# Attention weights split on VectorE, queries rotated out of PSUM, and another order of the first steps

## The chip, the cores and the metric

The kernel runs on one core of a Trainium2 chip. Its engines work beside each other, each through a fixed list of instructions: TensorE (PE, with its weight loads PEld) multiplies, VectorE (DVE), ScalarE (ACT) and GpSimd (POOL) work elementwise, and SyncE (SP) issues most transfers from memory. TensorE writes PSUM banks, from which VectorE and ScalarE read; everything else lies in SBUF. The metric is the device time of one execution in microseconds (us), as a median of several runs.

## What is computed

Two layers of a diffusion backbone over 512 latent tokens and 256 context tokens of width 1024, all in float32. Each layer modulates and normalises its input, projects it once, runs three mixers (attention, a short gated convolution, a longer convolution), merges them, and adds an MLP. The part that the change touches is modulation, projection and attention:

```python
sh1, sc1, gt1, sh2, sc2, gt2 = modulation(c, w_mod[l], b_mod[l])   # silu(c) @ w_mod + b_mod
h_lat = rmsnorm(x, g_norm1[l]) * (1.0 + sc1) + sh1
h_ctx = rmsnorm(ctx, g_norm1[l]) * (1.0 + csc1) + csh1
p_lat = h_lat @ w_in[l]
...
q_lat = apply_rope(query_heads(p_lat, q_gain[l]), cos, sin)   # 8 heads of 128, rmsnorm, rotation
k_lat, v_lat = keys_values(p_lat[..., OFF_K:OFF_SC], k_gain[l])   # 2 heads
k_lat = apply_rope(k_lat, cos, sin)
attn_lat = latent_attention(q_lat, k_lat, v_lat, k_ctx, v_ctx)   # one softmax over latent and context keys
x_new = x + gt1 * mixer_merge(p_lat, attn_lat, lp)
```

Context tokens run through the same weights; in the last layer only their keys and values are wanted.

## The kernel before

**Products in three passes.** Every float32 product is made of two-part operands: a high part rounded to TensorE's fp32r format and a low part, the rest. `mm3` (lines 152 to 156) issues high by high (L154), low by high (L155) and high by low (L156), into one bank. Weights come in units of 128 x 1024 values (512 KB). `unit` loads one into `wraw` (L121 or L123, four buffers), casts the high part on ScalarE (L125) and subtracts it for the low part on `self.lo_engine` (L127). That engine is GpSimd from the start, VectorE for V's weights and in part of a layer's rest, GpSimd again for others; in attention the four units of the first query group and the keys, and the six of the later query groups, go to GpSimd. Activations are split in the same way by `split` (ScalarE L147, VectorE or GpSimd L150).

**The first steps.** `first_modulation` makes the modulation of layer 0 in four quarters: eight loads of `w_mod` (L244, 256 KB each), products on one row (L250), a copy (L253), transposes (L256), and on VectorE the sums and the scale (L261, L263, L264). Quarter q serves the channel blocks k = 2q and 2q + 1. The blocks of x are read (L1057), squared on ScalarE (L1022), the root taken on GpSimd (`rstd`, L349 and L350) and scaled on VectorE (L1024). `modulate` transposes a channel block (L381) and evicts it with scale and shift on ScalarE (L386, L389) and VectorE (L391, L392). `qk_gemm_all` runs over k = 0 to 7, with `first_in` as the generator that is pulled ahead of each k. Its rope tables and gains are read and multiplied by `rotary` (L414, L419, L420). Layer 1 does the same from `next_in`, while layer 0's MLP ends.

**Attention.** `attention` makes keys and the first query group for the latents, then for the context, then V, then the queries of groups 1 to 3 in between the scores of the group before. A query pair comes from `qk_gemm` into one of four PSUM banks `pb`, is copied to SBUF (L405), squared on ScalarE (L457), and for latent pairs multiplied twice with the rope table on VectorE (L467) and added (L470). Each group has a third pair, the context's, in layer 0 only; it is multiplied with the gain alone (L460). Keys are then scaled on GpSimd (L500); for queries GpSimd makes the factor (L508, L510), which the softmax applies (L603 maximum, L604, L606 exponential, L607, L611). `to_heads` transposes a pair (L479). TensorE's transposes of probabilities are L625, its products with V L639 to L642.

**Order.** A scheduler fixes each engine's order ahead of the run from the program's order and its own estimates; at run time each engine works strictly through it and waits at the first instruction whose data or buffer is not there. SBUF tiles `tx` have 12 buffers, `pb` four banks here, `pa` two of double size.

Of the kernel before, what the change touches and what calls it, by code (L numbers as in the profile page):

```python
# [53 lines left out]
class Backbone:  # L54
    def __init__(self, ctx, tc, ins, out):
# [9 lines left out]
        self.lo_engine = tc.nc.gpsimd  # L65
# [50 lines left out]
    def unit(self, src, shape):  # L116
        nc = self.nc
# [4 lines left out]
        else:  # L122
            nc.sync.dma_start(out=raw, in_=src)  # L123
        hi = self.W("whi", N_SPLIT, shape, F32R)
# [274 lines left out]
    def qk_gemm(self, ws, hs, p):  # L399
        nc = self.nc  # L400
        ps = self.PB()
        for b in range(2):
            self.gemm_tm(ps[:, b * 256:(b + 1) * 256], ws, hs, 2 * p + b)
        t = self.X(512)
        nc.scalar.copy(t, ps)  # L405
        return t

    def rotary(self, l):

        nc, i = self.nc, self.i  # L410
        gains = []
# [4 lines left out]
        ropes = []  # L416
        for g in gains:
            rope = self.X(D)
            nc.sync.dma_start(out=rope, in_=i["rope"])  # L419
            nc.vector.tensor_tensor(rope.rearrange("p (q d) -> p q d", d=P), rope.rearrange("p (q d) -> p q d", d=P),  # L420
                                    g[:, None, :].broadcast_to([P, 8, P]), op=ALU.mult)
            ropes.append(rope)
        self.tables = gains, ropes

    def w_qk(self, w, u):

        src = w[u * 256:(u + 1) * 256, 0:2 * D].rearrange("(k p) (s c) -> p k s c", p=P, s=2)
        hi, lo = self.unit([src[:, k, :, 0:256] for k in range(2)], [2, 512])
# [22 lines left out]
    def qk_pair(self, ps, p, gain, rope):  # L451

        nc = self.nc
        t, t2 = ps, self.X(512)
# [7 lines left out]
        else:  # L462
            t1 = self.X(512)
            v = "p (b h d) -> p b h d"
            for dst, o in ((t1, 0), (t2, 512)):
                tab = rope[:, o + 2 * p * P:o + (2 * p + 2) * P].rearrange("p (b d) -> p b d", b=2)
                nc.vector.tensor_tensor(dst.rearrange(v, b=2, h=2), t.rearrange(v, b=2, h=2),  # L467
# [18 lines left out]
    def attention(self, l, hs, full, coming):  # L486
# [17 lines left out]
        def query(g, t, p):  # L504
            qt, qr = qs[g]
            t, ss = self.qk_pair(t, p, gains[1], ropes[1])
# [35 lines left out]
        self.lo_engine = nc.vector  # L542

        def v_heads():
            ws = self.w_rows(w, 0, OFF_V, 256)
            self.lo_engine = nc.gpsimd
# [13 lines left out]
        def queries(g):  # L560
# [3 lines left out]
            for p in range(3 if full else 2):  # L564
                query(g, self.qk_gemm(ws, hs, p), p)
# [182 lines left out]
    def layer(self, l, hs, x_src, full, last, coming):  # L748
# [208 lines left out]
        for c in range(N_FF // FF_CHUNK):  # L957
# [9 lines left out]
            for q, (h, blocks) in enumerate(orders):  # L967
# [3 lines left out]
                if q == 3:  # L971
                    self.lo_engine = nc.gpsimd
# [75 lines left out]
    def run(self):  # L1048
# [5 lines left out]
        def read(blocks):  # L1054
            xs = [self.X() for _ in blocks]
            for b, x in zip(blocks, xs):
                nc.sync.dma_start(out=x, in_=x_in(b))  # L1057
            for b, x in zip(blocks, xs):
                self.norm_in(b, x, x, self.X())

        self.read_ctx = lambda: read(range(NB_L, NB))
        self.first_cols = self.setup_cols(0)
        next(self.first_cols)
        self.quarters = [self.first_modulation(q) for q in range(4)]
        next(self.quarters[0])
        read(range(NB_L))
# [14 lines left out]
    def first_in(self, ws):  # L1081

        w = self.i["w_in"][0]
        quarters = self.quarters
        ws += self.w_qk(w, 0)
        next(quarters[1])
# [3 lines left out]
        for q in range(4):  # L1090
            if q < 2:
                next(quarters[q + 2])
            if q < 3:
# [79 lines left out]
```

## Time and profile before

| what | value |
|---|---|
| median of 3 runs | 2751.07 us (2750.91 to 2751.28) |
| the profiled execution | 2751.03 us |
| its span in the trace | 2749.2 us |
| TensorE busy | 2688.0 us (98%) |
| VectorE, ScalarE, GpSimd busy | 1625.3, 882.2, 760.5 us |
| mean granted clock of TensorE | 0.992 |

The trace covers 1.83 us less than the execution's own time. A line number is that of the kernel's file. A wait is idle time of an engine, put down to the instruction that released it last. The granted clock is given as a share of 2.4 GHz.

### The profile page before, as it was taken

The page shows a single profiled execution, that of the slowest core. Times are in us where ns is not written, and L with a number is a line of the kernel's source. Part 1 is how long each engine was busy: PE and PEld are TensorE (multiplying, and loading weights), DVE is VectorE, ACT ScalarE, POOL GpSimd, SP SyncE. Part 2 cuts the span into 40 slices and gives each one's busy share as a digit, 9 for nine tenths or more (in the row PEclk, how much of TensorE's full clock was granted, in tenths as well). Part 3 has the DMA queues.
Part 4 walks back from the last instruction along what each step waited for, and adds up shares of the span by engine and source line. Part 5 has one row for each costly group of instructions (what it writes and reads, how often), then busy time and mean ns, then how long its engine had stood idle before and what let it go on. Part 6 is the DMA issues. An engine that isn't in the chain of part 4 may idle for free.

```text
span 2749.2 us, 36048 instructions
## 1 busy us (share of the span) xinstructions
PE 2688.0 (98%) x14515; PEld 2302.1 (84%) x14515; DVE 1625.3 (59%) x2061; ACT 882.2 (32%) x1437; POOL 760.5 (28%) x621
## 2 busy tenths in 40 slices
PE   7899999999999999999999998999999999999998
PEld 4899888888888888888888887898888888888887
DVE  4557698538664434575454555667928735654445
ACT  3566222122221423412121225663223223422223
POOL 2543332233221231211110105535444212211102
PEclk9999999999999999999999999999999999999999
DMA  7111334422265243343343432113433534433332
GB/s 251 48 43 42 102 98 131 154 71 74 75 220 163 60 142 96 95 130 108 116 125 105 149 106 91 54 39 115 123 116 107 170 115 144 131 100 92 108 93 99
DMA packets 341982, 302.50 MB, mean 110 GB/s; under 512 B 10576, under 2 KB 288384, under 8 KB 341816
## 3 DMA queue, kind: packets, MB, share of 16 engines
q1 hardware_dynamic: 340400, 298.81, 35.0%
q8 instruction: 114, 1.87, 0.3%
q10 hardware_dynamic: 1416, 1.39, 0.2%
q14 instruction: 52, 0.43, 0.1%
HBM read 274.96 MB, written 25.20 MB: 109 GB/s over the span
## 4 chain that ended last, share of the span: by engine, by line
PE 89%; DVE 3%; issue 2%; ACT 1%; POOL 1%; DMA 1%; POOLq 0%; ACTq 0%; SPq 0%; DVEq 0%
PE pa L154 20%; PE pa L155 20%; PE pa L156 20%; PE pb L154 8%; PE pb L156 8%; PE pb L155 8%; PE pb L625 1%; PE pb L639 1%; PE pb L642 1%; PE pb L640 1%; DVE tx L295 1%; DMA wraw<-in_w_mod 1%; PE pb L303 1%; PE pb L479 0%; ACT tx L457 0%
## 5 line engine op out<-in xcount | busy, mean ns | idle before, releaser
L154 PE MATMUL pa<-ta,whi 128*128 128x512 f32 (+1 forms) x2912 | 1030.3, 354 | 0.8 <-DVE ta L788 0.8
L155 PE MATMUL pa<-ta,wlo 128*128 128x512 f32 (+1 forms) x2912 | 1026.1, 352 | 0.0
L156 PE MATMUL pa<-ta,whi 128*128 128x512 f32 (+1 forms) x2912 | 1025.2, 352 | 0.0
L125 ACT CAST whi<-wraw 128x1024 fp32r<-128x1024 f32 x360 | 377.6, 1050 | 1055.9 <-PE pa L156 391.6
L154 PEld LDWEIGHTS pa<-ta,whi 128*128 128x128 f32 x2912 | 551.3, 189 | 79.9 <-issue 3.4
L156 PEld LDWEIGHTS pa<-ta,whi 128*128 128x128 f32 x2912 | 550.8, 189 | 75.4 <-DVE ta L392 0.2
L155 PEld LDWEIGHTS pa<-ta,wlo 128*128 128x128 f32 x2912 | 551.4, 189 | 73.7
L127 POOL TENSOR_TENSOR wlo<-wraw,whi 128x1024 fp32r<-128x1024 f32 x138 | 334.9, 2432 | 407.4 <-ACT whi L125 358.5
L154 PE MATMUL pb<-whi,ta 128*128 128x512 f32 (+1 forms) x1200 | 434.6, 364 | 2.8 <-ACT ta L386 1.3
L155 PE MATMUL pb<-whi,ta 128*128 128x512 f32 (+1 forms) x1200 | 433.8, 361 | 2.3 <-DVE ta L392 1.8
L156 PE MATMUL pb<-wlo,ta 128*128 128x512 f32 (+1 forms) x1200 | 432.9, 361 | 1.4 <-DVE wlo L127 1.4
L707 DVE SCALAR_TENSOR_TENSOR pv<-tx,cols,pv 128x783 f32<-128x783 f32 (+1 forms) x448 | 401.2, 896 | 13.8
L127 DVE TENSOR_TENSOR wlo<-wraw,whi 128x1024 fp32r<-128x1024 f32 x222 | 294.6, 1329 | 83.6 <-ACT whi L125 78.1
L920 POOL TENSOR_TENSOR ta<-ta 128x768 fp32r<-128x768 f32 (+1 forms) x64 | 105.6, 1651 | 626.6 <-DVE ta L919 626.6
L154 PEld LDWEIGHTS pb<-whi,ta 128*128 128x128 f32 x1200 | 227.4, 190 | 41.9 <-ACT ta L386 3.0
L155 PEld LDWEIGHTS pb<-whi,ta 128*128 128x128 f32 x1200 | 227.7, 190 | 36.6 <-DVE ta L392 3.1
L156 PEld LDWEIGHTS pb<-wlo,ta 128*128 128x128 f32 x1200 | 227.2, 190 | 35.4 <-DVE wlo L127 1.9
L295 DVE SCALAR_TENSOR_TENSOR tx<-wraw,cs,tx 128x1024 f32<-128x1024 f32 x112 | 151.8, 1379 | 69.7 <-DMA wraw<-in_w_mod 64.7
L1045 DVE TENSOR_TENSOR ta<-pb,gt 128x512 f32<-128x512 f32 x100 | 68.8, 688 | 181.1 <-PE pb L156 181.0
L917 DVE TENSOR_SCALAR ta<-pa 128x768 f32<-128x768 f32 (+1 forms) x64 | 52.7, 823 | 165.2 <-PE pa L156 165.2
L745 ACT ACTIVATE ta<-pa 128x768 f32<-128x768 f32 (+1 forms) x52 | 36.6, 705 | 232.6 <-PE pa L156 232.6
L150 POOL TENSOR_TENSOR ta<-tx,ta 128x768 fp32r<-128x768 f32 (+1 forms) x32 | 53.6, 1674 | 158.4 <-ACT ta L147 154.0
(167 smaller groups left out, 2373.8 us busy)
## 6 DMA issues: line engine op xcount, KB each, us to landing
wraw<-in_w_in SPq DMA_DIRECT2D x144, 512.0 KB
wraw<-in_w_mod SPq DMA_DIRECT2D x80, 512.0 KB
wraw<-in_w_mlp_out SPq DMA_DIRECT2D x72, 512.0 KB
wraw<-in_w_mlp_in SPq DMA_DIRECT2D x64, 512.0 KB
wraw<-in_w_o SPq DMA_DIRECT2D x24, 512.0 KB
tx<-spill SPq DMA_DIRECT2D x24, 384.0 KB
ta<-in_w_mod SPq DMA_DIRECT2D x32, 256.0 KB
wraw<-in_w_attn_out SPq DMA_DIRECT2D x16, 512.0 KB
```

The costliest lines, as they stand in the source:

```text
L125: nc.scalar.copy(hi, raw)
L127: self.lo_engine.tensor_tensor(lo, raw, hi.bitcast(F32), op=ALU.subtract)
L150: (eng or nc.gpsimd).tensor_tensor(lo, src, hi.bitcast(F32), op=ALU.subtract)
L154: nc.tensor.matmul(ps, ah, bh, start=start, stop=False)
L155: nc.tensor.matmul(ps, al, bh, start=False, stop=False)
L156: nc.tensor.matmul(ps, ah, bl, start=False, stop=stop)
L295: nc.vector.scalar_tensor_tensor(acc[b], raw, c, acc[b], op0=ALU.mult, op1=ALU.add)
L707: nc.vector.scalar_tensor_tensor((v if t == K_CF - 1 else pv)[:, 0:n], u[:, t:t + n], c["cf"](t, k), (v if t == 1 else pv)[:, 0:n], op0=AL ...
L745: self.nc.scalar.activation(g[:, 0:n], ps[:, 0:n], AF.Sigmoid)
L917: nc.vector.tensor_scalar(out=v[:, 0:n], in0=ps[:, 0:n], scalar1=0.0, scalar2=None, op0=ALU.max)
L920: nc.gpsimd.tensor_tensor(lo[:, 0:n], v[:, 0:n], hi[:, 0:n].bitcast(F32), op=ALU.subtract)
L1045: nc.vector.tensor_tensor(t, ps, gt[:, o], op=ALU.mult)
```

## The change

It has four parts.

1. `lo_engine` is VectorE from the start, and no longer set to GpSimd behind V's weights: 20 L127 of attention (ten in each layer) move from GpSimd to VectorE.
2. `qk_gemm` returns the bank. The 15 copies L405 (nine in layer 0, six in layer 1) are gone; squares, rotation and the gain's multiply of these pairs read PSUM, and the result goes to a new tile.
3. SyncE reads x ahead of `w_mod`, each of the four first units of `w_in` ahead of its quarter (the first ahead of quarter 0), and both context blocks ahead of quarter 3. Before, x stood behind quarter 0, units two and three behind quarter 2, the fourth behind quarter 3, and one context block on either side of quarter 3.
4. `unit` is two functions, `load` and `halves`, and `rotary` two, so that loads are issued ahead of their splits and of the gain's multiply.

```diff
         self.bg = []
-        self.lo_engine = tc.nc.gpsimd
+        self.lo_engine = tc.nc.vector
         self.n = 0
...
     def unit(self, src, shape):
+        return self.halves(self.load(src, shape), shape)
+    def load(self, src, shape):
         nc = self.nc
...
             nc.sync.dma_start(out=raw, in_=src)
+        return raw
+    def halves(self, raw, shape):
+        nc = self.nc
         hi = self.W("whi", N_SPLIT, shape, F32R)
...
             self.gemm_tm(ps[:, b * 256:(b + 1) * 256], ws, hs, 2 * p + b)
-        t = self.X(512)
-        nc.scalar.copy(t, ps)
-        return t
+        return ps
-    def rotary(self, l):
+    def rotary_in(self, l):
         nc, i = self.nc, self.i
-        gains = []
+        gains, ropes = [], []
         for name in ("k_gain", "q_gain"):
...
             gains.append(g)
-        ropes = []
         for g in gains:
...
             nc.sync.dma_start(out=rope, in_=i["rope"])
-            nc.vector.tensor_tensor(rope.rearrange("p (q d) -> p q d", d=P), rope.rearrange("p (q d) -> p q d", d=P),
-                                    g[:, None, :].broadcast_to([P, 8, P]), op=ALU.mult)
             ropes.append(rope)
...
+    def rotary(self):
+        nc = self.nc
+        for g, rope in zip(*self.tables):
+            nc.vector.tensor_tensor(rope.rearrange("p (q d) -> p q d", d=P), rope.rearrange("p (q d) -> p q d", d=P),
+                                    g[:, None, :].broadcast_to([P, 8, P]), op=ALU.mult)
     def w_qk(self, w, u):
...
         src = w[u * 256:(u + 1) * 256, 0:2 * D].rearrange("(k p) (s c) -> p k s c", p=P, s=2)
-        hi, lo = self.unit([src[:, k, :, 0:256] for k in range(2)], [2, 512])
+        return self.load([src[:, k, :, 0:256] for k in range(2)], [2, 512])
+    def qk_halves(self, raw):
+        hi, lo = self.halves(raw, [2, 512])
         return [(hi[:, k], lo[:, k]) for k in range(2)]
...
-    def qk_pair(self, ps, p, gain, rope):
+    def qk_pair(self, ps, p, gain, rope, apart=False):
         nc = self.nc
-        t, t2 = ps, self.X(512)
+        t, t2 = self.X(512) if apart else ps, self.X(512)
         ss = self.st()
...
                 tab = rope[:, o + 2 * p * P:o + (2 * p + 2) * P].rearrange("p (b d) -> p b d", b=2)
-                nc.vector.tensor_tensor(dst.rearrange(v, b=2, h=2), t.rearrange(v, b=2, h=2),
+                nc.vector.tensor_tensor(dst.rearrange(v, b=2, h=2), ps.rearrange(v, b=2, h=2),
                                         tab[:, :, None, :].broadcast_to([P, 2, 2, P]), op=ALU.mult)
...
-        def query(g, t, p):
+        def query(g, t, p, apart=False):
             qt, qr = qs[g]
-            t, ss = self.qk_pair(t, p, gains[1], ropes[1])
+            t, ss = self.qk_pair(t, p, gains[1], ropes[1], apart)
             m = self.st()
...
-        self.lo_engine = nc.vector
         def v_heads():
             ws = self.w_rows(w, 0, OFF_V, 256)
-            self.lo_engine = nc.gpsimd
             for p in range(3):
...
             for p in range(3 if full else 2):
-                query(g, self.qk_gemm(ws, hs, p), p)
+                query(g, self.qk_gemm(ws, hs, p), p, True)
                 yield True
...
                     at = h
-                if q == 3:
-                    self.lo_engine = nc.gpsimd
                 for b in blocks:
...
                 nc.sync.dma_start(out=x, in_=x_in(b))
+            yield True
             for b, x in zip(blocks, xs):
                 self.norm_in(b, x, x, self.X())
+            yield True
-        self.read_ctx = lambda: read(range(NB_L, NB))
+        lat, self.read_ctx = read(range(NB_L)), read(range(NB_L, NB))
         self.first_cols = self.setup_cols(0)
         next(self.first_cols)
+        next(lat)
         self.quarters = [self.first_modulation(q) for q in range(4)]
-        next(self.quarters[0])
-        read(range(NB_L))
+        self.qk_raws = []
+        for q in range(2):
+            self.qk_raws.append(self.w_qk(i["w_in"][0], q))
+            next(self.quarters[q])
+        next(lat)
         next(self.first_cols)
...
         w = self.i["w_in"][0]
-        quarters = self.quarters
-        ws += self.w_qk(w, 0)
-        next(quarters[1])
+        quarters, raws = self.quarters, self.qk_raws
+        ws += self.qk_halves(raws[0])
         next(quarters[0])
...
             if q < 2:
+                raws.append(self.w_qk(w, q + 2))
                 next(quarters[q + 2])
-            if q < 3:
-                ws += self.w_qk(w, q + 1)
+            if q == 1:
+                next(self.read_ctx)
+                self.rotary_in(0)
             self.hs += self.new_pairs(2)
...
             next(self.lat)
-            if q == 1:
-                self.read_ctx()
-            if q == 2:
-                self.rotary(0)
             if q < 3:
+                ws += self.qk_halves(raws[q + 1])
                 next(quarters[q + 1])
             else:
-                run_all(self.first_cols)
+                next(self.read_ctx)
                 ctx = self.ctx_in(0)
...
                 next(quarters[q + 1])
+            else:
+                self.rotary()
+                run_all(self.first_cols)
             yield True
...
         l = DEPTH - 1
-        for u in range(KT // 2):
-            ws += self.w_qk(self.i["w_in"][l], u)
-        self.rotary(l)
+        raws = [self.w_qk(self.i["w_in"][l], u) for u in range(KT // 2)]
+        self.rotary_in(l)
+        for raw in raws:
+            ws += self.qk_halves(raw)
+        self.rotary()
         ctx = self.ctx_in(l)
```

New line numbers: L127 is now L134, L125 L132, L386 and L391 L393 and L398, L420 L431, L460 L473, L467 L480, L470 L483, L479 L492, L500 L513, L603 L613.

ScalarE in the first steps, behind the small loads of constants; L1022 are x's squares, L125 casts of weights, L386 and L389 the evictions of k = 0, 1. Before:

```order
L1022 ACTIVATE tx,st<-tx 128x1024 x4
L221 DMA tx<-in_w_cf_conv 124x128
L222 DMA tx<-in_w_cf_conv 124x128
L125 CAST whi<-wraw 128x1024
L386 ACTIVATE ta<-pa,mc_91,scale_93 128x512 x2
L389 ACTIVATE ta<-pa,mc_91,scale_93 128x512
L125 CAST whi<-wraw 128x1024 x2
L386 ACTIVATE ta<-pa,mc_91,scale_93 128x512
L1022 ACTIVATE tx,st<-tx 128x1024
L386 ACTIVATE ta<-pa,mc_91,scale_93 128x512
```

After:

```order
L1030 ACTIVATE tx,st<-tx 128x1024 x4
L228 DMA tx<-in_w_cf_conv 124x128
L229 DMA tx<-in_w_cf_conv 124x128
L132 CAST whi<-wraw 128x1024 x3
L393 ACTIVATE ta<-pa,mc_91,scale_93 128x512 x2
L396 ACTIVATE ta<-pa,mc_91,scale_93 128x512
L132 CAST whi<-wraw 128x1024
L393 ACTIVATE ta<-pa,mc_91,scale_93 128x512 x2
L396 ACTIVATE ta<-pa,mc_91,scale_93 128x512
```

Three casts now stand ahead of the first eviction, where it was one, and the fourth ahead of k = 2's.

VectorE at layer 0's first third pair; L460 is the gain's multiply, L150 the low part of transposed probabilities and other evictions, L603 the softmax maximum. Before:

```order
L150 TENSOR_TENSOR tx<-pb,tx 128x512
L604 TENSOR_SCALAR st<-st,qr 128x1
L607 RECIPROCAL st<-st 128x1
L603 TENSOR_REDUCE st<-pa 128x1
L460 TENSOR_TENSOR tx<-tx,gain 128x512
L150 TENSOR_TENSOR tx<-pb,tx 128x512
L604 TENSOR_SCALAR st<-st,qr 128x1
L150 TENSOR_TENSOR tx<-pb,tx 128x512
```

After (L473 is the multiply, L134 the splits, L157 and L613 as L150 and L603):

```order
L157 TENSOR_TENSOR tx<-pb,tx 128x512
L617 RECIPROCAL st<-st 128x1
L134 TENSOR_TENSOR wlo<-wraw,whi 128x1024 x2
L473 TENSOR_TENSOR tx<-pb,gain 128x512
L157 TENSOR_TENSOR tx<-pb,tx 128x512
L613 TENSOR_REDUCE st<-pa 128x1
L157 TENSOR_TENSOR tx<-pb,tx 128x512
L614 TENSOR_SCALAR st<-st,qr 128x1
```

Two splits of weights now stand ahead of the multiply, and the multiply reads PSUM.

GpSimd at the keys of layer 1; L500 scales a key's four parts, L349 and L350 take its root, the last four L500 are the context key's. Before:

```order
L349 TENSOR_SCALAR st<-st 128x4
L350 TENSOR_TENSOR st<-st,nhalf 128x4
L508 TENSOR_SCALAR st<-st 128x4
L510 TENSOR_TENSOR qr<-st,nhalf 128x4
L500 TENSOR_SCALAR tx<-tx,st 128x128 x4
L127 TENSOR_TENSOR wlo<-wraw,whi 128x1024
L349 TENSOR_SCALAR st<-st 128x4
L350 TENSOR_TENSOR st<-st,nhalf 128x4
L127 TENSOR_TENSOR wlo<-wraw,whi 128x1024
L500 TENSOR_SCALAR tx<-tx,st 128x128 x4
L611 TENSOR_SCALAR tx<-tx,st 128x768
L508 TENSOR_SCALAR st<-st 128x4
```

After:

```order
L356 TENSOR_SCALAR st<-st 128x4
L357 TENSOR_TENSOR st<-st,nhalf 128x4
L521 TENSOR_SCALAR st<-st 128x4
L523 TENSOR_TENSOR qr<-st,nhalf 128x4
L513 TENSOR_SCALAR tx<-tx,st 128x128 x4
L356 TENSOR_SCALAR st<-st 128x4
L357 TENSOR_TENSOR st<-st,nhalf 128x4
L513 TENSOR_SCALAR tx<-tx,st 128x128 x4
L621 TENSOR_SCALAR tx<-tx,st 128x768
L521 TENSOR_SCALAR st<-st 128x4
L523 TENSOR_TENSOR qr<-st,nhalf 128x4
```

Both splits between the second key and the context key are gone from this queue.

## Rows read from the trace of the kernel before

**Rows 1.** The page: busy time, share and instructions of each engine.

```profile
PE 2688.0 (98%) x14515; PEld 2302.1 (84%) x14515; DVE 1625.3 (59%) x2061; ACT 882.2 (32%) x1437; POOL 760.5 (28%) x621
```

**Rows 2.** TensorE's waits: engine, tile, line, released by; total us, times, longest.

```profile
PE pb L479 <- POOL tx L500: 9.2, 6, 4.4
...
PE pb L479 <- DVE tx L470: 2.8, 3, 1.6
...
PE pa L155 <- DVE ta L392: 1.3, 1, 1.3
...
PE pa L381 <- DVE ta L391: 1.2, 1, 1.2
```

**Rows 3.** Busy by stretch: PE, PEld, DVE, ACT, POOL; granted clock, DMA share, GB/s.

```profile
18.00:28.00 10.00, 4.76 (x19) 1.95 (x23) 6.38 (x11) 2.98 (x4) 4.74 (x5) 0.51 1.11 341
1690.00:1720.00 30.00, 23.85 (x170) 22.60 (x170) 11.32 (x24) 11.51 (x38) 16.29 (x21) 0.89 0.19 57
1720.00:1750.00 30.00, 26.56 (x174) 24.80 (x174) 19.11 (x36) 17.54 (x41) 19.01 (x14) 0.89 0.24 70
1706.10:1711.20 5.10, 5.10 (x26) 5.10 (x25) 0.00 (x0) 0.00 (x0) 0.00 (x0) 0.51 0.27 92
```

**Rows 4.** Groups by line and shape: busy us, mean ns, idle before.

```profile
L127 POOL TENSOR_TENSOR wlo<-wraw,whi 128x1024 fp32r<-128x1024 f32 x138 | 334.9, 2432 | 407.4 <-ACT whi L125 358.5 <-issue 42.9 <-DVE pv L707 5.3
L127 DVE TENSOR_TENSOR wlo<-wraw,whi 128x1024 fp32r<-128x1024 f32 x222 | 294.6, 1329 | 83.6 <-ACT whi L125 78.1 <-PE pb L155 0.3
...
L150 DVE TENSOR_TENSOR tx<-pb,tx 128x512 fp32r<-128x512 f32 x104 | 70.3, 685 | 13.7 <-ACT tx L147 13.4
...
L457 ACT ACTIVATE tx<-tx 128x128 f32<-128x128 f32 x104 | 30.9, 301 | 0.9
...
L470 DVE TENSOR_TENSOR tx<-tx 128x512 f32<-128x512 f32 x20 | 13.7, 686 | 0.1
...
L405 ACT COPY tx<-pb 128x512 f32<-128x512 f32 x15 | 8.8, 585 | 25.8 <-PE pb L156 17.4 <-issue 8.5
```

**Rows 5.** Timeline of the start: start us, duration us, engine, line [idle before].

```profile
20.74 2.88 DVE L1024 TENSOR_SCALAR tx<-tx,st 128x1024 f32<-128x1024 f32 x1 [0.72 <-POOL st L350]
...
26.18 0.78 ACT L386 ACTIVATE ta<-pa,mc,scale 128x512 fp32r<-128x512 f32 x1 [5.53 <-DVE scale L264]
...
35.74 1.04 ACT L125 CAST whi<-wraw 128x1024 fp32r<-128x1024 f32 x1 [0.43 <-DMA wraw<-in_w_in]
...
49.95 1.23 DVE L420 TENSOR_TENSOR tx<-tx,gain 128x1024 f32<-128x1024 f32 x1
...
28.88 1.19 PE L154 MATMUL pb<-whi,ta 128*128 128x512 f32 x4
...
50.97 0.96 PE L154 MATMUL pb<-whi,ta 128*128 128x512 f32 x3 [1.26 <-ACT ta L386]
```

**Rows 6.** Timeline of layer 0's first third pair (VectorE, GpSimd, TensorE).

```profile
143.27 0.96 DVE L603 TENSOR_REDUCE st<-pa 128x1 f32<-128x768 f32 x1 [4.37 <-PE pa L156]
144.37 2.05 DVE L460 TENSOR_TENSOR tx<-tx,gain 128x512 f32<-128x512 f32 x1
...
141.12 4.75 POOL L127 TENSOR_TENSOR wlo<-wraw,whi 128x1024 fp32r<-128x1024 f32 x2 [1.22 <-ACT whi L125]
...
147.16 0.63 PE L479 MATMUL pb<-ident,tx 128*128 128x128 f32 x4 [1.47 <-DVE st L604]
```

**Rows 7.** Timeline at the ctx key of layer 1 (GpSimd, TensorE).

```profile
1698.59 2.39 POOL L127 TENSOR_TENSOR wlo<-wraw,whi 128x1024 fp32r<-128x1024 f32 x1
...
1705.08 0.48 PE L479 MATMUL pb<-ident,tx 128*128 128x128 f32 x1 [4.43 <-POOL tx L500]
```

**Rows 8.** Timeline of layer 1's second query pair (VectorE, TensorE).

```profile
1738.47 2.72 DVE L467 TENSOR_TENSOR tx<-tx 128x512 f32<-128x512 f32 x1
...
1739.78 0.49 PE L154 MATMUL pa<-ta 128*128 128x512 f32 x1 [1.82 <-ACT tx L606]
...
1742.71 1.12 PE L479 MATMUL pb<-ident,tx 128*128 128x128 f32 x4 [1.62 <-DVE tx L470]
```

More of the change, by code (lines that the diff above doesn't have):

```diff
@@ L419, in rotary @@
             nc.sync.dma_start(out=rope, in_=i["rope"])
+            ropes.append(rope)
+        self.tables = gains, ropes
+    def rotary(self):
+        nc = self.nc
+        for g, rope in zip(*self.tables):
             nc.vector.tensor_tensor(rope.rearrange("p (q d) -> p q d", d=P), rope.rearrange("p (q d) -> p q d", d=P),
                                     g[:, None, :].broadcast_to([P, 8, P]), op=ALU.mult)
-            ropes.append(rope)
-        self.tables = gains, ropes
     def w_qk(self, w, u):
         src = w[u * 256:(u + 1) * 256, 0:2 * D].rearrange("(k p) (s c) -> p k s c", p=P, s=2)
-        hi, lo = self.unit([src[:, k, :, 0:256] for k in range(2)], [2, 512])
+        return self.load([src[:, k, :, 0:256] for k in range(2)], [2, 512])
+    def qk_halves(self, raw):
+        hi, lo = self.halves(raw, [2, 512])
         return [(hi[:, k], lo[:, k]) for k in range(2)]
```

## The prediction

> **What bounds the kernel now.** I read the page first: TensorE is busy 2688.0 of 2749.2 us [rows 1], so only 61.2 us of its idle time can be won, and the work it does is not changed. The list of TensorE's waits comes next [rows 2], to see which idle times end with something that the change touches: key heads waiting for GpSimd's multiply L500 (9.2 us in six waits, 4.4 in the longest), the pairs of heads waiting for VectorE's rotation L470, two waits behind the splits L392 and L391. Then the table by stage with the granted clock [rows 3]: in 18 to 28 us and 1706.1 to 1711.2 us the clock is 0.51, that is 1.2 GHz and not 2.4, and both follow idle time of TensorE; 1690 to 1750 us is the poorest stretch after the start, 50.41 us busy in 60. Next the prices by line and form [rows 4], last the timelines of four places [rows 5 to 8].
>
> What they show together: whenever GpSimd runs L127 (2.43 us a split [rows 4]), a VectorE operation with two SBUF operands that starts meanwhile ends with it. L1024 takes 2.88 us at 20.74 [rows 5], L460 takes 2.05 at 144.37 beside a 4.75 us pair of splits [rows 6], L467 takes 2.72 at 1738.47 [rows 8], where L470, of the same size, takes 0.69 on average [rows 4]. The trace has some ten such places.
>
> **The splits (20 from GpSimd to VectorE).** Removed on GpSimd: 20 x 2.43 = 49 us; added on VectorE: 20 x 1.33 = 27 us [rows 4]. VectorE is busy 11.32 and 19.11 us in the two stretches of 30 us from 1690 to 1750 [rows 3], so the room is there; what counts is who stands behind each. By place:
> - Layer 0's third pairs. TensorE waits 1.47 us at 147.16 behind L460, L150 and L604 [rows 6]; three such waits of 1.46 to 1.47. Now both splits stand ahead of the multiply L473. The first cast is ready at 141.1, when GpSimd starts, the second some 1.4 us later, and VectorE idles 4.37 us up to 143.27 [rows 6], so both splits are done at about 143.8, before the squares are over; the multiply takes 0.7 and not 2.05. What is left of each wait is about 0.3: -3.4 us.
> - ctx stage: the 1.3 us wait behind a stretched L392 [rows 2] goes, the V weights' splits come a little later: -1.0.
> - Boundary to layer 1: four splits in a row go from GpSimd; the 1.2 us behind L391 [rows 2] falls to 0.3: -0.9.
> - The ctx key of layer 1. GpSimd does a split, a norm, a split, and only then the four multiplies L500; TensorE waits 4.43 + 0.21 us [rows 7]. Without the two splits (2.39 and one like it) the multiplies come some 4.7 us sooner, and the order puts their transposes behind all V products as well: -4.6. The half clock follows this wait: 25 matmuls took 5.1 us there [rows 3], at full clock half, and some transposes: -3.0. I take both, since nothing else waits between 1698 and 1711.
> - 1735 to 1744 us: waits of 1.82 and 1.62 [rows 8]. The first is a softmax row maximum queued on VectorE. With the change a split (1.33) and both rotations (1.37) stand ahead of it, so it comes about 1.2 us later, while the rotated pair comes about 3 us sooner. Worked along the queue, idle falls from 3.4 to about 2.5: -1.0, and a quarter chance that the half clock of this stretch (0.89 over 30 us [rows 3], so 3.3 us lost at most) stays away: -0.7.
> - The later pairs (two waits of 1.15, the same pattern): -1.0.
>
> **Rotating out of PSUM.** 15 copies L405 of 0.585 us go from ScalarE [rows 4]. VectorE reading one PSUM operand of this size takes 0.685 (L150), both operands in SBUF 0.686 (L470) [rows 4], so I take no price; the squares at 0.301 each were timed from SBUF only; the 512-column copy from PSUM needs 0.585 for four times the columns, so the bounds are 0 to +0.1 each, hidden either way. The Trainium skill's page "VectorE: DVE Perf Modes" (Rules for kernel authors) says one should either accept the slower tier of a PSUM source or copy to SBUF first where many operations follow; three readers follow here. By it the rotation would cost more than 0.69, and the sum would rise by under 1 us for each pair; the rows of this kernel don't agree, at this size and type.
>
> The price lies elsewhere: the bank. It was free after the copy, 0.7 us; now it is free after four squares (1.3) and two rotations (1.37), which the order puts behind the squares: about 2.85 us. Four banks rotate. Counting matmuls in the new order at 0.06, 0.12 and 0.23 us for 128, 256 and 512 columns (25 of mostly 256 columns take 5.1 us at half clock [rows 3]), TensorE has 2.2 to 3.7 us of work before the bank comes round in seven of nine pairs of layer 0 (8.2 in the first, 3.1 in the second), 4.9 in four of layer 1, 2.8 and 16.5 in the others. Beyond the cover lie 0.65 + 0.65 + 0.05; with a split now and then ahead: **+2.0**. Bounds 0, and +21 with a cast (1.05) and a split (1.33) ahead of every one.
>
> **The start.** x first, each w_in unit ahead of its quarter. The stretched L1024 (2.88, [rows 5]) goes, and x is normed before the first quarter is there. Against that, ScalarE's and VectorE's order have the third unit's cast and split ahead of k=0's evictions. That unit landed at 35.7 [rows 5] and has 2 MB fewer ahead of it: 5.9 us at 341 GB/s [rows 3], and I estimate 1.7 us more since the big x transfers fill the queues sooner (0 to 3). So 28.2, cast 1.04, eviction 0.78: first product at 30.0 and not 28.88 [rows 5]; with the split and VectorE's two evictions the second kind of product is 1.7 us late. Later it wins: the stretched operations and waits at 40 to 54 us go (1.26 at 50.97 [rows 5], and some of like size). The products L431 (1.23 each, as L420 [rows 5]) now stand ahead of the third quarter's scale, and wait for the rope tables: 14.1 MB at 341 GB/s from about 5 us, 46 to 47; the scale is ready at about 49 and k=4 starts at 50.0, 1.0 before. If TensorE's clock, 0.51 until 28 us [rows 3], stays low over the first 7 us of products, 3.5 us are lost. I take **0**, between -4 (all lands sooner, clock as before) and +5.
>
> **Sum**: 0 - 1.0 - 3.4 + 2.0 - 0.9 - 7.6 - 1.7 - 1.0 = -13.6. The profiled execution took 2751.03 us, its span 2749.2 and 1.83 around it, and the median is 2751.07, so either base serves: **2737 us**.
>
> **Rivals.**
> - *The bank becomes the wait* (the slower side). In every query pair the squares find a cast ahead and the rotations a split: 5.2 us against the covers above is +21 in place of +2; the pairs' own waits (3.4) don't go, since the same queues cause them: 2737.4 + 19 + 3.4 = 2760. It decides from 1.4 us beyond the cover per pair, over 15. For it: VectorE and ScalarE work in program order and get the splits there. Against: only ten splits of a layer lie there, and VectorE idles 4.37 us ahead of the third pair [rows 6].
> - *The start and the clock don't give*: +4 at the start, and 3.0 + 0.7 of clock time not returned as other idle time of 2 us keeps TensorE slow at 1706: 2745. For it: the row of 18 to 28 us; against: no wait between 1692 and 1705 but the one that goes.
> - *The blocking turns round*: VectorE's splits now stretch GpSimd's small operations in the ctx key's chain, three times 1.33, and the clock gives back nothing there: 2737.4 + 4 + 3 = 2744. The rows show VectorE held up by GpSimd; the reverse is not among them. The Trainium skill states it as a lock: on "SBUF — State Buffer" (SBUF: two separate sides), the pair of ports that VectorE's two-operand instructions and GpSimd share goes to whichever starts first, for the whole instruction. By that rule the splits on VectorE can hold GpSimd as well; the trace agrees for the other direction, with L460's 2.05 us beside GpSimd's splits.
> - *All of it comes*: the start's -4 and both half-clock stretches: 2731.
>
> **How the numbers follow.** Forecast 0.45, all of it 0.17, start and clock 0.17, blocking 0.14, bank 0.07. The measurement tells 0.2% (5.5 us) from no change: faster is under 2745.6, slower over 2756.6. Faster: 0.45 + 0.17, half of the start rival and three quarters of the blocking one: 0.81. Slower 0.05, from the bank; the rest 0.14. The range leaves out the bank rival's far end and the best tenth: 2727 to 2750.
>
> **What would show it.** No DVE operation of two SBUF operands and 512 columns over 1 us in attention; the wait of 4.43 at the ctx key gone and the clock at 1.0 there; waits before third pairs of 0.3; TensorE's first product at about 30 us and k=4 at about 50. It is wrong if TensorE waits for L480 (bank) over 1 us in most pairs, if the ctx key's transposes still wait, or if the start is over 5 us longer.

## The result, and the profile after

The changed kernel took **2731.82 us** (median of four, 2730.98 to 2733.03) against 2751.18 (2750.91 to 2751.65): a ratio of 0.9931, with a 95% interval of 0.9918 to 0.9943. That is 19.4 us less, where 13.6 were forecast, inside the range of 2727 to 2750. The profiled execution's span is 2730.0 us against 2749.2.

The page of the changed kernel, busy time by engine, answers to [rows 1]:

```profile
PE 2682.9 (98%) x14515; PEld 2298.2 (84%) x14515; DVE 1625.6 (60%) x2081; ACT 871.7 (32%) x1422; POOL 709.2 (26%) x601
```

TensorE does the same 14515 matmuls in 5.1 us less, which I put down to the clock (the windows below), and stands idle 47.1 us and not 61.2, which is waits: 14.1 + 5.1 = 19.2, the difference of the spans. TensorE's waits, for [rows 2]:

```profile
PE pb L492 <- POOL tx L513: 4.6, 4, 1.9
...
PE pb L492 <- DVE tx L483: 1.5, 1, 1.5
```

L492 and L513 are L479 and L500 of before: 9.2 us in six waits became 4.6 in four. The stretches of [rows 3] (windows: PE, PEld, DVE, ACT, POOL; granted clock, DMA share, GB/s):

```profile
18.00:28.00 10.00, 6.30 (x27) 2.10 (x29) 2.45 (x7) 1.04 (x1) 0.00 (x0) 0.73 0.99 321
1690.00:1720.00 30.00, 29.97 (x234) 28.64 (x234) 17.51 (x37) 14.39 (x36) 12.26 (x19) 1.00 0.23 70
1720.00:1750.00 30.00, 28.15 (x213) 26.18 (x212) 21.63 (x46) 18.78 (x50) 9.76 (x12) 1.00 0.19 57
```

The 60 us from 1690 are now 58.12 us busy, at full clock. Prices by line and shape, for [rows 4]:

```profile
L134 DVE TENSOR_TENSOR wlo<-wraw,whi 128x1024 fp32r<-128x1024 f32 x242 | 319.5, 1322 | 107.4 <-ACT whi L132 101.5 <-DMA tx<-spill 0.3 <-PE pb L162 0.3
L134 POOL TENSOR_TENSOR wlo<-wraw,whi 128x1024 fp32r<-128x1024 f32 x118 | 285.0, 2418 | 381.9 <-ACT whi L132 332.8 <-issue 44.0 <-DVE pv L717 4.4
...
L480 DVE TENSOR_TENSOR tx<-pb,tx 128x512 f32<-128x512 f32 x24 | 15.4, 685 | 32.7 <-ACT tx L470 27.6 <-POOL wlo L134 5.0
...
L483 DVE TENSOR_TENSOR tx<-tx 128x512 f32<-128x512 f32 x20 | 13.9, 693 | 0.1
```

Twenty splits moved; the rotation out of PSUM (L480) costs 0.685 us, as priced. The timelines that answer to [rows 5], [rows 6], [rows 7] and [rows 8] (start, duration, engine, line, idle before):

```profile
28.59 1.04 ACT L132 CAST whi<-wraw 128x1024 fp32r<-128x1024 f32 x1 [6.53 <-DMA wraw<-in_w_in]
29.54 0.77 ACT L393 ACTIVATE ta<-pa,mc,scale 128x512 fp32r<-128x512 f32 x1
...
30.36 0.73 PE L161 MATMUL pb<-whi,ta 128*128 128x512 f32 x2 [1.24 <-ACT ta L393]
...
52.34 0.96 PE L161 MATMUL pb<-whi,ta 128*128 128x512 f32 x3 [1.10 <-ACT ta L393]
```

```profile
139.94 1.23 DVE L134 TENSOR_TENSOR wlo<-wraw,whi 128x1024 fp32r<-128x1024 f32 x1 [2.70 <-ACT whi L132]
141.38 1.23 DVE L134 TENSOR_TENSOR wlo<-wraw,whi 128x1024 fp32r<-128x1024 f32 x1 [0.22 <-ACT whi L132]
142.52 0.68 DVE L473 TENSOR_TENSOR tx<-pb,gain 128x512 f32<-128x512 f32 x1
...
143.92 0.60 PE L492 MATMUL pb<-ident,tx 128*128 128x128 f32 x4
...
185.82 4.76 POOL L134 TENSOR_TENSOR wlo<-wraw,whi 128x1024 fp32r<-128x1024 f32 x2 [1.21 <-ACT whi L132]
```

```profile
1696.40 1.41 POOL L513 TENSOR_SCALAR tx<-tx,st 128x128 f32<-128x128 f32 x4
...
1697.25 1.47 PE L492 MATMUL pb<-ident,tx 128*128 128x128 f32 x12
...
1722.77 1.30 DVE L134 TENSOR_TENSOR wlo<-wraw,whi 128x1024 fp32r<-128x1024 f32 x1 [0.78 <-ACT whi L132]
1723.99 1.27 DVE L480 TENSOR_TENSOR tx<-pb,tx 128x512 f32<-128x512 f32 x2
...
1726.79 0.66 PE L492 MATMUL pb<-ident,tx 128*128 128x128 f32 x4 [1.47 <-DVE tx L483]
```

The third pair's transposes (143.92) and the ctx key's (1697.25) no longer wait at all; one pair in layer 1 still does, 1.47 us, and one in layer 0, 0.92 (before: 1.0). The line at 185.82 shows that GpSimd still splits weights beside layer 0's second third pair. By place, from the shift of the same TensorE instruction between the two traces: the start **+0.3** us, the rest of layer 0's attention **-5.4**, from there to layer 1 **+0.4**, the boundary and layer 1's attention **-14.6**. Of these 14.6, 7.6 lie at the ctx key, some 4 at the pair that waited at 1739 to 1743 us before, and 2.4 at the later pairs.

### The profile page after: what moved, and what is told of

Same layout as the page of the kernel before. It is cut to its first block, busy times and chain, and to the rows that moved or that the text cites. A ratio compares the mean times of both kernels' runs of the same rounds, so it can differ in the third digit from the quotient of the medians.

```text
span 2730.0 us, 36072 instructions
## 1 busy us (share of the span) xinstructions
PE 2682.9 (98%) x14515; PEld 2298.2 (84%) x14515; DVE 1625.6 (60%) x2081; ACT 871.7 (32%) x1422; POOL 709.2 (26%) x601
## 3 DMA queue, kind: packets, MB, share of 16 engines
q10 hardware_dynamic: 1416, 1.39, 0.2%
## 4 chain that ended last, share of the span: by engine, by line
PE 90%; DVE 3%; DMA 3%; issue 2%; POOL 1%; ACT 1%; SPq 0%; POOLq 0%; DVEq 0%; ACTq 0%
PE pa L161 20%; PE pa L162 20%; PE pa L163 20%; PE pb L161 8%; PE pb L163 8%; PE pb L162 8%; PE pb L635 2%; DMA wraw<-in_w_mod 1%; PE pb L649 1%; DVE tx L302 1%; PE pb L652 1%; PE pb L650 1%; DMA ta<-in_w_mod 1%; PE pb L310 0%; PE pa L388 0%
## 5 line engine op out<-in xcount | busy, mean ns | idle before, releaser
L132 ACT CAST whi<-wraw 128x1024 fp32r<-128x1024 f32 x360 | 377.7, 1051 | 1068.1 <-issue 385.9
L134 POOL TENSOR_TENSOR wlo<-wraw,whi 128x1024 fp32r<-128x1024 f32 x118 | 285.0, 2418 | 381.9 <-ACT whi L132 332.8
L134 DVE TENSOR_TENSOR wlo<-wraw,whi 128x1024 fp32r<-128x1024 f32 x242 | 319.5, 1322 | 107.4 <-ACT whi L132 101.5
L157 POOL TENSOR_TENSOR ta<-tx,ta 128x768 fp32r<-128x768 f32 (+1 forms) x32 | 53.6, 1674 | 157.3 <-ACT ta L154 152.8
```

The costliest lines, as they stand in the source:

```text
L132: nc.scalar.copy(hi, raw)
L134: self.lo_engine.tensor_tensor(lo, raw, hi.bitcast(F32), op=ALU.subtract)
L157: (eng or nc.gpsimd).tensor_tensor(lo, src, hi.bitcast(F32), op=ALU.subtract)
```

## The experiments

Ratios stand against runs of the kernel before on the same chip, with 95% intervals; the changed kernel's is 0.9931.

**1 and 2. Each part alone.** `splits_only` is the kernel before with the changed engine for 20 splits, `psum_only` the kernel before with the rotation out of PSUM:

```
splits_only, in attention:        psum_only:
+ self.lo_engine = nc.vector      - t = self.X(512); nc.scalar.copy(t, ps); return t
...                               + return ps
+ self.lo_engine = nc.gpsimd      + t, t2 = self.X(512) if apart else ps, self.X(512)
```

> The kernel before with the first part of the change alone: 20 weight splits of attention on VectorE, none of the rest. Theory A (GpSimd's splits hold up VectorE and its own key multiplies, and that is the whole gain): 2733 us, within 3 of the changed kernel; the 4.43 us wait at layer 1's ctx key is gone, the granted clock is 1.00 from 1690 to 1750 us, the three waits of 1.46 us at layer 0's third pairs are gone. Rival B (the copies on ScalarE are in the same chains, so splits alone bring half): 2740 to 2745 us, with the waits at third pairs left at about 1 us.

> The kernel before with the second part alone: the 15 copies out of PSUM left out, later queries rotated from the bank, splits still on GpSimd. Theory A: 2750 us, within 2 of the kernel before: the rotation waits for the squares now, which takes what the copy gave, and VectorE is still held up beside GpSimd's splits. Rival B: 2744 us or less. Rival C (the bank held longer is a wait): 2753 us or more, with TensorE waiting for VectorE's second rotation.

Measured: 2736.29 us, ratio 0.9953 (0.9938 to 0.9968), and 2740.30 us, 0.9966 (0.9953 to 0.9978). The second third pair of layer 0, in splits_only and then in psum_only (timelines), and psum_only's ctx key:

```profile
184.55 4.74 POOL L127 TENSOR_TENSOR wlo<-wraw,whi 128x1024 fp32r<-128x1024 f32 x2 [1.21 <-ACT whi L125]
...
187.87 1.98 DVE L460 TENSOR_TENSOR tx<-tx,gain 128x512 f32<-128x512 f32 x1
...
190.60 0.63 PE L479 MATMUL pb<-ident,tx 128*128 128x128 f32 x4 [1.47 <-DVE st L601]
```

```profile
186.65 4.75 POOL L127 TENSOR_TENSOR wlo<-wraw,whi 128x1024 fp32r<-128x1024 f32 x2 [1.21 <-ACT whi L125]
...
189.14 0.69 DVE L458 TENSOR_TENSOR tx<-pb,gain 128x512 f32<-128x512 f32 x1 [4.70 <-PE pa L156]
...
190.48 0.66 PE L477 MATMUL pb<-ident,tx 128*128 128x128 f32 x4
...
1699.12 1.41 POOL L498 TENSOR_SCALAR tx<-tx,st 128x128 f32<-128x128 f32 x4
...
1699.55 0.47 PE L477 MATMUL pb<-ident,tx 128*128 128x128 f32 x1 [4.40 <-POOL tx L498]
```

Both kernels have GpSimd's pair of splits at that place, 4.74 us. Beside it the multiply of two SBUF operands takes 1.98 us and TensorE waits 1.47; the multiply of one PSUM operand takes 0.69 and nobody waits. So the splits at two of layer 0's three third pairs, and at layer 1's later ones, aren't among the 20 (they are the next phase's weights), and what removed those waits is the operand. Neither run came out as one theory had it: splits_only lies between A and B, since two of the three third-pair waits stay at 1.46 to 1.47 us; psum_only comes in as rival B. The ctx key is the reverse: its 4.40 us stay with psum_only and go with splits_only. The two parts alone give 13.7 and 9.7 us, 23.4, and together 19.4: the first third pair's wait (1.47) is gone in both, and so is the half clock from 1720 us (0.89 before, 1.00 in both), so these are counted twice.

**3 and 4. The start alone, and all but the start.**

```
start_only: before + x read first, units and quarters in the new order
no_start:   after, but with before's order of the first steps
```

> The kernel before with the third and fourth part alone: x read first, units ahead of their quarters, loads apart from splits; splits on GpSimd, copies kept. Theory A: 2751 us, within 2 of the kernel before, since k=4 starts about 1 us later and a wait or two behind it go. Rival D (the first steps gain, and VectorE's splits there give it back): 2746 us, first product at 28 us.

> Splits on VectorE and queries out of PSUM, with the first steps as in the kernel before. Theory A: 2731 us, within 1.5 of the changed kernel, either side. Rival D: 2736 us or more, since the start would carry 4 us or so.

Measured: 2750.54 us, 1.0005 (0.9996 to 1.0014), and 2730.74 us, 0.9934 (0.9919 to 0.9948). The start is worth nothing either way.

**5. The copy stays, and only the rotations read PSUM.** In psum_only ScalarE's copy also goes. Here it stays, for the squares:

```
+ t, t2 = self.X(512) if apart else ps, self.X(512)
+ if apart:
+     nc.scalar.copy(t, ps)
...
-                 nc.vector.tensor_tensor(dst.rearrange(v, b=2, h=2), t.rearrange(v, b=2, h=2),
+                 nc.vector.tensor_tensor(dst.rearrange(v, b=2, h=2), ps.rearrange(v, b=2, h=2),
```

> The kernel before, splits on GpSimd; the 15 copies stay, squares read the copy, but the rotation and the gain's multiply read the PSUM bank. The run with the second part alone gained 9.7 us. Theory L (a VectorE instruction is held up beside GpSimd's split only where both its operands lie in SBUF; an operand in PSUM frees it): most of it stays, 6 to 9 us, so 2741 to 2744, and the rotations take 0.7 us beside GpSimd's splits. Rival S (it is the copy on ScalarE, ahead of the squares): 2749 us or more.

Measured: 2739.07 us, 0.9960 (0.9947 to 0.9973). All instructions of line L467, the rotations' multiplies (minimum, median, maximum ns), in the kernel before and then here:

```profile
L467 DVE TENSOR_TENSOR tx<-tx x40: 677/692/2720, 67.9 to 1813.6; 128x512 f32<-128x512 f32 x40
```

```profile
L467 DVE TENSOR_TENSOR tx<-pb,tx x24: 678/691/693, 112.5 to 1804.5; 128x512 f32<-128x512 f32 x24
L467 DVE TENSOR_TENSOR tx<-tx x16: 678/682/776, 67.2 to 1688.5; 128x512 f32<-128x512 f32 x16
...
1732.83 4.74 POOL L127 TENSOR_TENSOR wlo<-wraw,whi 128x1024 fp32r<-128x1024 f32 x2
...
1736.72 1.39 DVE L470 TENSOR_TENSOR tx<-tx 128x512 f32<-128x512 f32 x1
```

Of the 24, six (layer 1's) overlap a split of GpSimd's in either trace. In the kernel before these six took 1.07 to 2.72 us; here, reading PSUM, 0.68 to 0.69. The trace has its own comparison: beside the pair of splits at 1732.83, two multiplies that read PSUM keep 0.68 and 0.69 us, and the add L470 behind them, with both operands in SBUF, takes 1.39. The gain of psum_only is all here, with the copy still in place: it is the operand's place that pays, not the copy saved.

**6. Only the two splits at the ctx key.**

```
+ if not full and g == 1:
+     self.lo_engine = nc.vector
...
+ self.lo_engine = nc.gpsimd
```

> The kernel before with only two of the 20 splits on VectorE: the weights of the first later query group of layer 1, which stand between the second key and the ctx key in GpSimd's queue. Theory K (the 4.43 us wait is GpSimd's queue, and the half clock behind it follows the wait): 7 to 8 us less than before, 2742 to 2743, granted clock 1.00 from 1690 to 1720 us, the stretch from 1720 on as before. Rival (the clock is low for another reason): 4.5 us less, and the clock at 0.5 for some 6 us there.

Measured: 2742.45 us, 0.9970 (0.9958 to 0.9982): 7.4 us from two splits, as the prediction's -4.6 and -3.0 had it. The granted clock is 1.00 from 1690 to 1720 us (0.89 before) and still 0.89 from 1720 to 1750.

**7 and 8. GpSimd's time given back.** To splits_only, work for GpSimd is added where its splits were: each difference once more in four quarters, into scrap (`dup_split`); or a tiny difference and eight memsets (`dup_memset`); a memset reads nothing from SBUF.

```
dup_split:  + for j in range(4):
            +     nc.gpsimd.tensor_tensor(scrap, rf[:, j * 256:(j + 1) * 256], hf[:, j * 256:(j + 1) * 256], op=ALU.subtract)
dup_memset: + nc.gpsimd.tensor_tensor(scrap[:, 0:2], rf[:, 0:2], hf[:, 0:2], op=ALU.subtract)
            + for j in range(8):
            +     nc.gpsimd.memset(scrap.bitcast(F32), 0.0)
```

> The run with the splits on VectorE alone, which took 13.7 us less than before; beside each of its 20 moved splits GpSimd now computes the same difference once more, in four quarters into a scrap tile that nobody reads. The results are the same. Theory L: GpSimd's two-operand reads hold VectorE up and stand in the ctx key's queue as before, so nearly all is lost: 2748 to 2751. Rival Q (only GpSimd's queue matters): the ctx key's wait and its clock come back, 2743 to 2745.

> As the run with duplicated splits, but GpSimd fills the scrap tile eight times with zeros in the same place of its queue, after a two-column difference that makes it wait for the same weights: about as long, and reading no SBUF. Theory L: only the queue's part comes back, 2741 to 2745, and no VectorE instruction beside the fills takes longer than alone. Rival W (any GpSimd work holds VectorE up, writes too): as the duplicated splits, within 2 us.

Measured: 2760.75 us, 1.0034 (1.0022 to 1.0047), and 2746.83 us, 0.9989 (0.9980 to 0.9999). GpSimd's groups, of dup_split (with minimum, median and maximum in ns) and then of dup_memset, the latter with one of TensorE's waits:

```profile
L133 POOL TENSOR_TENSOR scrap<-wraw,whi 128x256 fp32r<-128x256 f32 x80 | 80.3, 1003 | 27.6 <-ACT whi L126 21.8 <-POOL scrap L133 0.3
...
L133 POOL TENSOR_TENSOR scrap<-wraw,whi x80: 722/742/1826, 20.6 to 1756.0; 128x256 fp32r<-128x256 f32 x80
```

```profile
L134 POOL MEMSET scrap<- 128x256 f32 x160 | 50.8, 317 | 8.8
...
L132 POOL TENSOR_TENSOR scrap<-wraw,whi 128x2 fp32r<-128x2 f32 x20 | 12.8, 639 | 23.9 <-ACT whi L126 23.0
...
PE pb L486 <- POOL tx L507: 6.8, 6, 1.9
```

The memsets occupy GpSimd about as long as the 20 splits did (50.8 against 49 us; the tiny differences add 12.8), and cost 10.5 us. VectorE's 512-column steps of two SBUF operands beside them kept their 0.67 to 0.69 us, so this cost is put down to GpSimd's queue; it is some 2 us more than theory L gave. The quarters cost 24.5. They don't give the two shares cleanly: the 80 pieces took 80.3 us, not 49, since a piece of 0.72 to 0.75 us takes up to 1.83 where VectorE's own split of two SBUF operands runs beside it, so dup_split's GpSimd is also later. Of its size the expectation was wrong by 10 us. That queue and blocking both cost is shown by key_splits and copy_kept, which change one and leave the other; these two runs agree, but don't give the shares.

**9. The bank held longer.** Four more ScalarE copies read the query bank between squares and rotations:

```
+ if apart:
+     for _ in range(4):
+         nc.scalar.copy(t2, ps)
```

> The changed kernel, and in each of the 15 later query pairs four more ScalarE copies (0.585 us each, 2.3 us) that read the query bank between the squares and the rotations, so that the bank is free about 5 us after its last matmul and not about 2.85. Theory B (the prediction's count of the cover, 2.2 to 3.7 us in most pairs of layer 0, is right, and the 2.0 us it charged went unnoticed somewhere else): TensorE waits for L480 or L470 at the next use of the bank, 1.3 to 2.8 us in some nine pairs, and each pair's own transposes wait too: 2748 to 2756. Theory C (the bank comes round later than was counted): no wait on the bank over 1 us in most pairs; only pairs' own transposes wait, where the four copies make the rotations late, at most 2.3 us in the six third pairs and a few others: 2733 to 2744.

Measured: 2760.97 us, 1.0042 (1.0027 to 1.0057): more than either theory's. TensorE's waits there (L495 is the pairs' and keys' transposes, L638 the probabilities', three lines on from L492 and L635):

```profile
PE pb L495 <- DVE tx L486: 7.1, 3, 3.8
...
PE pb L495 <- DVE st L617: 5.2, 3, 3.2
...
PE pb L638 <- DVE st L617: 3.4, 2, 1.7
PE pb L638 <- DVE ta L157: 2.3, 3, 0.8
```

No wait names a reader of the query bank (the squares L470, the copies L474, the multiplies L483), though by the trace it is held 5.0 to 6.1 us after its last matmul, against 2.5 to 3.4 in the changed kernel. The waits for a bank that do show are behind the softmax's exponential (L619), 1.4 us in four. So the bank comes round later than the prediction counted; how late isn't measured, since TensorE's other waits here push its next use back as well. What held VectorE ahead of the multiplies L483 (us, times):

```profile
  ACT tx L474: 14.0, 10
```

The cost, 29 us in all, goes through the queues: VectorE stands at the rotation until the copies are done, and behind it the softmax's small steps and the pair's own transposes come late; and ScalarE's own queue is 2.3 us longer in each pair. What share each queue has isn't shown. In this run the late rotation cost, and the held bank did not.

**10 and 11. Can the start give anything?** Layer 0's first four units are cast and split on GpSimd, and its gain products L431 done there too; `gp_late` also asks for unit and quarter one step later.

```
+ nc.gpsimd.tensor_copy(hi, raw)   (first four units; the split likewise)
+ (nc.vector if self.l1 else nc.gpsimd).tensor_tensor(rope.rearrange("p (q d) -> p q d", d=P), rope.rearrange("p (q d) -> p q d", d=P),
```

> The changed kernel, but the first four w_in units of layer 0 are cast and split on GpSimd (idle there) and layer 0's two gain products L431 too; order of code unchanged. Theory S (the start loses because the third unit's cast stands ahead of the first evictions on ScalarE, and its split ahead of them on VectorE): the first product comes at 26 to 28 us and not 30.4, and the time is 2727 to 2731. Theory T (the start is set by what lands, x, the scale and the units, and TensorE's slow clock follows any early product): first product earlier, but the fifth kind of product stays at 51 to 53 us, and the time stays at 2731 to 2734. If GpSimd's splits hold up VectorE's two-operand steps of the start, it is over 2734.

> As the run before, and the third and later units and quarters are asked for and emitted in the order in which the products use them (unit and quarter of a step behind the products of the step before). Theory S: first product at about 26 us, k=4 at 42 to 46 us, time 2725 to 2729. Theory T: k=4 stays at 50 us or later, since the rope tables and the scale's quarters set it, time 2731 or more.

Measured: 2737.23 us, 0.9958 (0.9941 to 0.9974), and 2738.13 us, 0.9962 (0.9947 to 0.9977), so 5.4 and 6.3 us above the changed kernel. The timeline of gp_first:

```profile
27.78 0.73 PE L165 MATMUL pb<-whi,ta 128*128 128x512 f32 x2
...
49.49 2.34 POOL L435 TENSOR_TENSOR tx<-tx,gain 128x1024 f32<-128x1024 f32 x1
...
49.56 2.82 DVE L1036 TENSOR_SCALAR tx<-tx,st 128x1024 f32<-128x1024 f32 x1 [4.84 <-POOL st L361]
...
54.22 1.12 PE L392 MATMUL pa<-ident,tx 128*128 128x128 f32 x4 [6.46 <-DVE ta L402]
```

The first product comes 2.6 us sooner (27.78, not 30.36), and then GpSimd's L435 holds VectorE's norm for 2.82 us in place of 0.75; the scale is made behind the norm, and TensorE waits 6.46 us. The fifth kind of product starts at 57.1, not 52.3. In gp_late it starts at 56.0. A sooner first product is worth nothing while that scale comes no sooner, and putting L431 on GpSimd brings back what the change took out. Since the units and L431 moved together, the units alone weren't tried.

**12. The key's multiplies on VectorE.** What waits are left at the keys end with GpSimd's L513:

```
- nc.gpsimd.tensor_scalar(out=t[:, q * P:(q + 1) * P], in0=t[:, q * P:(q + 1) * P],
+ nc.vector.tensor_scalar(out=t[:, q * P:(q + 1) * P], in0=t[:, q * P:(q + 1) * P],
```

> The changed kernel, but the key heads' four multiplies by the reciprocal norm (L513, 24 in the program) are done on VectorE and not on GpSimd. In the changed kernel GpSimd takes 1.41 us for four where VectorE is idle, and 3.27 us (at 72.6) and 5.41 us (at 1681.3) where VectorE works from SBUF operands beside it; TensorE waits for them 1.89 and 1.16 us at 74 to 76 and 0.65 and 0.86 us at 1685 to 1687. Theory R (the blocking goes both ways, and these 4.6 us are what it costs TensorE): four multiplies on VectorE take about 0.8 to 1.2 us, the four waits fall to 1.5 us or less together, and the time is 2727 to 2729.5. Theory Q (VectorE's queue takes its place: splits and rotations ahead of the multiplies): the waits move to L513 on VectorE and keep 3 us or more, 2730 to 2734, or over 2734 if VectorE's other readers (row maxima, evictions) are late behind it.

Measured: 2742.40 us, 0.9962 (0.9948 to 0.9976), some 10 us above the changed kernel (its five runs lie between 2736.4 and 2745.4, and the slowest is the profiled one). The line, TensorE's waits, and the stretch from 1690 us:

```profile
L513 DVE TENSOR_SCALAR tx<-tx,st x24: 274/281/288, 71.6 to 1700.1; 128x128 f32<-128x128 f32 x24
...
PE pa L388 <- DVE ta L398: 7.7, 3, 5.2
...
PE pb L163 <- DVE wlo L134: 4.4, 4, 1.9
...
1690.00:1720.00 30.00, 25.25 (x188) 23.96 (x186) 17.59 (x37) 11.95 (x42) 11.19 (x9) 0.94 0.22 71
```

Four multiplies take 0.86 us, and the waits behind L513 are gone. But VectorE, in program order, now stands at L513 until GpSimd's root (L357) is done (4.7 us in five places), and behind it wait the evictions (L398) and the splits. The longest wait, 5.2 us at layer 0's keys, costs little, since the 3.0 us behind L513 are gone there: at 81 us the kernel is 0.9 us behind the changed one. Most is lost at layer 1's keys, where it falls from 2.6 us behind at 1658 us to 10.9 at 1705: TensorE waits 2.0, 0.8, 1.9 and 2.1 us there, and its clock is 0.94 and not 1.00. That is theory Q, its second case. No version tried beats the changed kernel; no_start equals it.

## Why the prediction was right, and where it was not

- **What bounds the kernel**: held. The gain is TensorE's waits (14.1) and clock (5.1), no work.
- **What GpSimd's split holds up**: held in the main, and read too loosely in two points. In [rows 6] the multiply doesn't end with the splits but 0.55 us after them, about what it needs alone (0.68). And L1024, which the prediction counts among operations of two SBUF operands, has one tensor and one scalar per partition: it too is held (2.88 us, and 2.82 beside L435 in gp_first, against 0.75).
- **The start, 0**: measured +0.3, and start_only and no_start agree. The first product was forecast at 30.0 and came at 30.36; k=4 at 50.0, 1.0 us sooner than before, and came at 52.34, 1.4 us later, since the norms of the context stand on VectorE between the steps of the scale as well as the products L431. What was lost was won back by 80 us, so the 0 is in part luck.
- **Layer 0's attention, -2.4 by the sum (-1.0, -3.4, +2.0)**: measured -5.4. Two steps failed here. "Now both splits stand ahead of the multiply" holds for the first of three third pairs only; the other two waits went because of the PSUM operand, to which the prediction gave "no price" and no gain. And the **bank's +2.0** is 0: the hold was sized well (2.85, measured 2.5 to 3.4), but no wait in the changed kernel names a reader of the query bank, nor does one in hold4, with a hold that the count said would cost 21. What failed is the cover of 2.2 to 3.7 us, counted too short.
- **Boundary and layer 1, -11.2**: measured -14.6. The ctx key's -4.6 and -3.0 are key_splits' 7.4 us. The clock, given a quarter's chance from 1720 us, came back there too: 1.00 in the third window, and the place gave some 4 us where -1.7 stood. The later pairs gave 2.4 where -1.0 stood: their waits went, by the operand again (copy_kept).
- **The reverse blocking**: the prediction said that it isn't among the rows. That is so of the rows it had chosen, but the trace of before has it. GpSimd's four L500 in three places of it, and VectorE beside the second:

```profile
1686.50 5.41 POOL L500 TENSOR_SCALAR tx<-tx,st 128x128 f32<-128x128 f32 x4
...
1697.21 1.42 POOL L500 TENSOR_SCALAR tx<-tx,st 128x128 f32<-128x128 f32 x4
1697.24 0.76 DVE L150 TENSOR_TENSOR ta<-pb,ta 128x256 fp32r<-128x256 f32 x2 [0.44 <-ACT ta L147]
...
1704.65 1.41 POOL L500 TENSOR_SCALAR tx<-tx,st 128x128 f32<-128x128 f32 x4
```

The same four multiplies take 1.41 us where VectorE has nothing to do, 1.42 where it works with one operand from PSUM (L150), and 5.41 where it works from two SBUF operands (L127, L467 and L470, from 1686.05 on). So the operand in PSUM spares GpSimd as well. The change doesn't make it worse on the path, as the rival feared (2744): beside a split of VectorE's (1692.43) one key's multiplies take 2.27 us, and nobody waits for them. The Trainium skill's page "SBUF — State Buffer" (SBUF: two separate sides) has one pair of ports that belongs to whichever starts first, for the whole instruction, and counts VectorE's two-input instructions only where both inputs are in SBUF and GpSimd's reads SBUF. The runs agree on each point: 1.98 us against 0.69 by the operand, no stretch beside memsets, and both directions.
- **The Trainium skill's page "VectorE: DVE Perf Modes"** (Rules for kernel authors), with its choice between a slower PSUM source and a copy first: measured 0.685 against 0.686 us at this size and type, so the price that the prediction read out of it didn't come; and beside GpSimd's splits the PSUM operand is the faster one.
- The time landed by "all of it comes" (2731), and only half by its reasons: both half-clock stretches came back, but the start gave nothing, and the operand made up for it. That part is luck.

## What to carry to other kernels

Where two engines block each other over SBUF, there are two remedies, and a trace prices both: move one engine's work, or take one operand of the other's from PSUM, which cost nothing here and worked at places where the first engine's work had to stay. Before an operation is moved to an engine that works in program order, look at what it will wait for there and who stands behind it: pieces of 0.86 us that wait cost some 10 us, and 2.3 us ahead of each of 15 rotations cost 29. When a shared queue is shown to be in the way, read the trace for both directions of it.

## What the runs showed of the hardware

- GpSimd's difference of two SBUF operands takes, undisturbed, 0.194 to 0.198 us for two columns (dup_memset) and 0.72 to 0.75 for 256 (dup_split), against 2.4 for 1024; beside VectorE's split it took up to 1.40 and 1.83. Four quarters of 0.73 are 2.9 us: cutting it costs about a fifth, and the rest of the mean of 1.00 us is blocking.
- A multiply of 128 columns by a scalar per partition takes 0.37 us on GpSimd with VectorE idle or reading PSUM, up to 1.59 us beside VectorE's work from two SBUF operands, and 0.28 us on VectorE.
- ScalarE's square of 128 columns took 0.276 us from PSUM and 0.304 from SBUF in the changed kernel: reading PSUM has no price there either.
- TensorE's clock in 18 to 28 us was 0.51 before, 0.73 after and 1.00 in start_only, whose time is that of before; it was 0.50 in no_start, whose time is that of the changed kernel: there the clock is not what sets the time.
